# Softmax reciprocals from GpSimd to VectorE, and one group of adaLN rows from the first channel mixer to the second token mixer

## The chip, the cores and the metric

The kernel runs on one core of a Trainium2 (trn2) chip. The metric is the device time of one execution in microseconds (us), and what counts is the median of several executions. In the text, TensorE, VectorE, ScalarE, GpSimd and SyncE are the five engines; the profile calls them PE (with PEld for its weight loads), DVE, ACT, POOL and SP.

## What is computed

Two layers of a conditioned decoder trunk run over 256 tokens of width 1024. All is fp32. Cut to its structure, the reference is:

```python
c_act = silu(c)
for l in range(2):
    mod = c_act @ w_mod[l] + b_mod[l]                      # six adaLN rows of 1024
    sh1, sc1, g1, sh2, sc2, g2 = split(mod, 6)
    h = rms_norm(x, mix_norm_g[l]) * (1 + sc1) + sh1
    x = x + g1 * token_mixer(h, ...)                       # attention A, attention B, conv, gates, w_out
    h = rms_norm(x, ffn_norm_g[l]) * (1 + sc2) + sh2
    x = x + g2 * channel_mixer(h, ...)                     # w_up, 3-tap conv, silu(a)*b, w_down
```

The token mixer projects `h` once and has three branches: a latent attention (8 heads), a second attention (8 heads, which with 256 tokens is plain causal attention), and a gated causal convolution of 31 taps over 512 channels. The three branches are weighted by sigmoid gates, summed and projected by `w_out`. Softmax divides each row of exponentials by its sum; the reciprocal of that sum is what the first part of the change is about. Row (l, r) below is the r-th of the six adaLN rows of layer l: (1,2) is `g1` of the second layer, the gate with which the token mixer's output is added to `x`.

## The kernel before

Tokens stand in the free dimension, channels on the 128 partitions, so `x` is eight tiles of 128x256. Products in fp32 are made of three matmuls each: both factors are split into a rounded part (hi, type fp32r) and the rest (lo), and hi·hi, lo·hi and hi·lo are accumulated in PSUM (lines 281 to 291).

Weights come in units of 512 KB. SyncE loads a unit to `raw` (line 194, 4 buffers), ScalarE rounds it to `whi` (line 211), VectorE subtracts to get `wlo` (line 213), and TensorE uses both. Units are taken three ahead of their use (`AHEAD = 3`).

Each engine executes its list of instructions in order. The lists follow from the order in which the program's parts are written, with a scheduler at build time that fixes each engine's list. The order of the parts in a token mixer is written out by hand in `STEPS`, one string for each layer. Of its names, `MA` and `BA` are parts of the two attentions, `C` and `G` gates, `O` and `OC` output products of the branches, `PR` the last projection. A pair in small letters marks a stretch over which a list of small pieces is spread evenly (`_spread`): `v0`..`v1` the conv taps, `m0`..`m1` parts of rows that are made by matmul, and `r0`..`r1` adaLN rows that VectorE makes.

An attention group (`attn4`, line 555) has four heads. TensorE makes the scores, VectorE takes the maxima (lines 582 and 584) and their scaled negatives `nb` (lines 588 and 591), ScalarE takes exponentials with their sums `sm` (line 604), and then comes the reciprocal of 128x4 sums, two for each group, 16 in all:

```python
ri = small(4, "ri", 4)
if RIP:
    gp.tensor_tensor(ri, sm, minus1[:, 0:4], op=ALU.pow)
```

ScalarE multiplies the probabilities with it (line 619), TensorE transposes them (line 628) and multiplies with the values (line 640), and the result is split to `oah`, `oal` or `obh`, `obl` (lines 643 and 644). The conv taps are VectorE operations of 128x256 (lines 1012 and 1015), which are spread among the attention groups.

An adaLN row (l, r) takes eight steps k. In each, SyncE loads 512 KB of `wmr` (line 366) and VectorE multiplies it by `crow`, which is silu(c) laid out over all partitions, and sums (line 371); a small addition of the bias follows (line 372). `crow` is made by `row_load`: a load (step `RW0`, line 1132), a tanh on ScalarE (line 1135) and a product on VectorE (line 1136, step `RW3`). It stands in the pool "kv" with 2 buffers, and in the token mixer the rows' loads have 2 buffers of the pool "qkT". In the kernel before, rows (0,3) and (0,4) are made in the first layer's token mixer (`RPARTS`), and rows (1,0), (1,1) and (1,2) in the first channel mixer.

The channel mixer has 22 groups of 256 columns. `up(j)` makes a group in PSUM (`psb`, 3 buffers, two units of weights), ScalarE takes it from there (line 1192), VectorE adds the taps (line 1194), and after the activation (lines 1199 and 1200) the product is split to `mh` and `ml` (lines 1202 and 1203). At its end stand the rows of the first layer:

```python
for _ in range(2 if j % 7 == 6 else j > 0):
    if rows_left:
        mod_row(crow1[0], *rows_left.pop(0), scale=0.5 if CDMA else 1.0)
```

There they have four loading buffers of their own. `down(j)` multiplies with the down weights, 24 matmuls to 48 in `up`, so 72 a group and 1584 in a channel mixer. `up` runs three groups ahead of `down`, and the last three `down` are issued together (`TAIL = 3`, lines 282 to 284). The new `x` follows from them (line 1226). `g1h` (line 1144) is where the second layer's token mixer uses row (1,2), after its last projection.

Of the kernel before, what the change touches and what calls it, by code (L numbers as in the profile page):

```python
# [9 lines left out]
F32 = mybir.dt.float32  # L10
# [4 lines left out]
ALU = mybir.AluOpType  # L15
AX = mybir.AxisListType

P = 128
S = 256
NB = 2  # L20
D = 1024
KD = 8
# [8 lines left out]
VFROM = [("QKV", 2, 0), ("KL", 0)]  # L31
TAPS = 4
SQP = 0
RIP = 1
LNAT = {"LN": 16, "LS": 18, "LB": 20}
PB = 4
DVN = ()
# [6 lines left out]
CDMA = 1  # L44
# [1 line left out]
HOLD = 0  # L46
SQ4 = 1
CHAIN = 1
RPARTS = [(0, 3), (0, 4)]
RFROM = ("G", 5, 0)  # L50
RTO = ("PR", 5)
MFROM = ("QKV", 2, 0)
# [3 lines left out]
LINE = 512  # L56
LEAD = 16
TAILP = 2
FLEAD = 1
ROWS = [(0, 0), (0, 1), (1, 0), (1, 1), (1, 2)] + RPARTS  # L60


PARTS = [[(0, r) for r in (2, 3, 4) if (0, r) not in RPARTS], [(1, 4)]]
# [19 lines left out]
)]  # L83


def _spread(o, items, first, last):

    i0, i1 = o.index(first), o.index(last)
    total = sum(UNITS.get(t[0], 0) for t in o[i0:i1])
    res, done, n = [], 0, 0  # L90
    for i, t in enumerate(o):
        res.append(t)
        if i0 <= i < i1:
            done += UNITS.get(t[0], 0)
            while n < len(items) and done >= total * (n + 0.5) / len(items) - 1e-9:
                res.append(items[n])
                n += 1
    return res


def _order(l):
    o = []
    for w in STEPS[l].split():
        name = w.rstrip("0123456789")
        o.append((name, *(int(d) for d in w[len(name):])))
    o = _spread(o, [("V", j, t, min(31, t + TAPS)) for j in range(4) for t in range(0, 31, TAPS)], ("v", 0), ("v", 1))
    if ("r", 0) in o:
        o = _spread(o, [("R", r, k) for _, r in RPARTS for k in range(KD)], ("r", 0), ("r", 1))
    o = _spread(o, [("M",)] * (9 * len(PARTS[l])), ("m", 0), ("m", 1))
    return [t for t in o if t[0].isupper() and not (l == 0 and C0K and t[:2] == ("C", 0))]  # L110

# [37 lines left out]
def trunk_kernel(ctx, tc, xT, crow, ccol, pos, invf, modb_d, cols_d, grow_d, wmr, wm, win1, wqkv,  # L149
                  wgc, wgab, wuq, wukv, woab, woc, wout, wup, wdn, out):  # L150
    nc = tc.nc
    te, ac, ve, gp, sy = nc.tensor, nc.scalar, nc.vector, nc.gpsimd, nc.sync

    cst = ctx.enter_context(tc.tile_pool(name="cst", bufs=1))
    per = ctx.enter_context(tc.tile_pool(name="per", bufs=1))
    wk = ctx.enter_context(tc.tile_pool(name="wk", bufs=2))
# [4 lines left out]
    def nm(s):  # L161
        uid[0] += 1
        return f"{s}_{uid[0]}"
# [149 lines left out]
    ve.memset(mean_w, 1.0 / 512.0)  # L313
    mhalf = cst.tile([P, 24], F32, name="mhalf")
    ve.memset(mhalf, -0.5)

    minus1 = cst.tile([P, 4], F32, name="minus1")
    ve.memset(minus1, -1.0)


    def silu_row(res, tag="thc", bufs=1):
# [53 lines left out]
    def mod_row(row, l, r, k, tag=None, scale=1.0):  # L375

        return use_row(wload_row(l, r, k, tag), row, l, r, k, scale)
# [177 lines left out]
    def attn4(qT, kT, v, scale, scq, oth, otl, oslot, apart=False):  # L555
# [39 lines left out]
        for i in range(2):  # L595
            sm = small(4, "smx", 4)
            ps = []
            for h in (2 * i, 2 * i + 1):
                pr = wk.tile([P, 384], F32, tag="p", name=nm("p"), bufs=PB)
                for b in range(NB):  # L600
                    src = (at0 if b == 0 else at1)[h]
                    at = h % 2 * 2 + i
                    dst = pr[:, 0:P] if b == 0 else pr[:, P:384]
                    ac.activation(dst, src, AF.Exp, bias=nb[:, b, at:at + 1],  # L604
                                  scale=scale if scq is None else scq[b][:, h:h + 1],
                                  accum_out=sm[:, len(ps):len(ps) + 1])
                    ps.append(dst)
            ri = small(4, "ri", 4)
            if RIP:
                gp.tensor_tensor(ri, sm, minus1[:, 0:4], op=ALU.pow)  # L610
            else:
                ve.reciprocal(ri, sm)
            prs.append((ps, ri))
        for ps, ri in prs:
            for n, pr in enumerate(ps):
# [54 lines left out]
    def layer(l):  # L670
# [455 lines left out]
        def row_load(n):  # L1126

            if not CDMA:
                return step(rowgen, 2 if n == 3 else 1)
            if n == 0:  # L1130
                crow1.append(wk.tile([P, D + 128], F32, tag="kv", name=nm("crow"), bufs=2, align_bytes=LINE)[:, 0:D])
                sy.dma_start(crow1[0], crow)
            elif n == 3:
                th = wk.tile([P, D], F32, tag="qkT", name=nm("th"), bufs=2, align_bytes=LINE)
                ac.activation(th, crow1[0], AF.Tanh, scale=0.5)
                ve.scalar_tensor_tensor(crow1[0], th, 1.0, crow1[0], op0=ALU.add, op1=ALU.mult)

        run["RW"] = row_load
        run["R"] = lambda r, k: mod_row(crow1[0], 0, r, k, "qkT", 0.5 if CDMA else 1.0)
        for tok in CFG["order"][l]:  # L1140
            run[tok[0]](*tok[1:])
        step(mods, 99)
# [19 lines left out]
            ve.tensor_scalar(fb[:, NF:44], cv(l, "fdw_b")[:, NF:44], 0.5, None, op0=ALU.mult)  # L1162
        acc2 = []
        acts = []
        rows_left = [(1, r, k) for r in range(3) for k in range(KD)] if l == 0 else []

        def down(j):
            if not acc2:
# [10 lines left out]
        def up(j):  # L1179
# [22 lines left out]
            ac.activation(mh, th, AF.Copy)  # L1202
            ve.tensor_tensor(ml, th, mh.bitcast(F32), op=ALU.subtract)
            acts.append((mh, ml))
            for _ in range(2 if j % 7 == 6 else j > 0):
                if rows_left:
                    mod_row(crow1[0], *rows_left.pop(0), scale=0.5 if CDMA else 1.0)
            if l + 1 < L and j == 6:
                load_cols(l + 1)
                prepare(l + 1)  # L1210
# [107 lines left out]
```

## Time and profile before

| | before |
|---|---|
| times of three runs | 961.74, 956.33, 953.44 us; median 956.33 |
| profiled execution | 960.24 us, of it span 958.4 us |
| mean granted clock of TensorE in the span | 0.979 |
| TensorE matmuls (PE) busy | 910.8 us, 95% |
| TensorE weight loads (PEld) busy | 852.6 us, 89% |
| VectorE (DVE) busy | 792.0 us, 83% |
| ScalarE (ACT) busy | 553.7 us, 58% |
| GpSimd (POOL) busy | 81.9 us, 9% |
| read from memory | 198.81 MB, mean 209 GB/s |

The span runs from the first to the last instruction of the profiled execution; times in the trace count from its start. The first layer's token mixer adds to `x` from 287.9 us on (line 1146), its channel mixer from 487.0 us (line 1226), and the last addition to `x` of the second token mixer starts at 757.3 us. Matmuls are pipelined, so a busy share near 100% says that TensorE isn't starved, not that it runs at its peak. The granted clock is given as a share of 2.4 GHz, so 0.5 is 1.2 GHz. Shares over the whole span mix stages with different limits, and so stretches of 10 to 40 us are read below.

### The profile page before, as it was taken

How to read it: one execution, taken by the hardware profiler on the slowest of the kernel's cores; microseconds unless marked ns; L12 is line 12 of the kernel's file. 1: busy time of each engine (PE TensorE's matmuls, PEld its weight loads, DVE VectorE, ACT ScalarE, POOL GpSimd, SP SyncE). 2: the span in 40 equal slices, each digit the busy share in tenths (PEclk: the TensorE clock that was granted, in tenths of full speed). 3: DMA queues.
4: the chain of work that ended last, by engine and by line, in shares of the span. 5: the costliest groups of instructions: out<-in, count | busy, mean ns of one | idle time of the engine just before them, and what ended most of it. 6: DMA issues, size and time to landing. Idle time of an engine off the chain costs nothing.

```text
span 958.4 us, 18539 instructions
## 1 busy us (share of the span) xinstructions
PE 910.8 (95%) x7262; PEld 852.6 (89%) x7262; DVE 792.0 (83%) x1524; ACT 553.7 (58%) x978; POOL 81.9 (9%) x48
## 2 busy tenths in 40 slices
PE   3999899799999999999899999979999999999998
PEld 2998788798997999999879987769999899999998
DVE  5999799799997899998874999967677798777774
ACT  4577488634655555555643675847565566555551
POOL 1011621300000000000000042231000000000000
PEclk9999999999998999999979999979999999999999
DMA  7966434388896878888753665505557767656641
GB/s 255 388 218 216 140 111 138 125 271 303 289 323 227 287 252 287 294 309 265 227 184 103 193 221 186 176 23 176 189 167 229 264 210 219 185 190 181 193 134 44
DMA packets 58120, 201.07 MB, mean 210 GB/s; under 512 B 6960, under 2 KB 8496, under 8 KB 58032
## 3 DMA queue, kind: packets, MB, share of 16 engines
q1 hardware_dynamic: 58032, 199.88, 62.4%
q8 instruction: 57, 0.93, 0.4%
q14 instruction: 31, 0.25, 0.1%
HBM read 198.81 MB, written 1.05 MB: 209 GB/s over the span
## 4 chain that ended last, share of the span: by engine, by line
PE 68%; DVE 11%; issue 8%; DMA 5%; POOL 4%; ACT 3%; SPq 0%; POOLq 0%; DVEq 0%; ACTq 0%
PE psb L288 13%; PE psb L291 13%; PE psb L289 13%; PE psa L288 6%; PE psa L289 6%; PE psa L291 6%; DVE wlo L213 3%; POOL rs L470 2%; DVE cacc L1015 2%; PE psa L388 2%; DMA raw<-in_wmr 2%; POOL ri L610 2%; ACT p L604 2%; DVE raw L371 1%; PE psa L628 1%
## 5 line engine op out<-in xcount | busy, mean ns | idle before, releaser
L211 ACT ACTIVATE whi<-raw 128x1024 fp32r<-128x1024 f32 (+2 forms) x286 | 294.4, 1037 | 217.0 <-PE psb L289 100.4
L213 DVE TENSOR_TENSOR wlo<-raw,whi 128x1024 fp32r<-128x1024 f32 (+2 forms) x286 | 340.4, 1194 | 82.6 <-ACT whi L211 71.4
L288 PE MATMUL psb<-hh,whi 128*128 128x256 f32 x1088 | 263.6, 283 | 1.2 <-ACT p L604 0.8
L289 PE MATMUL psb<-hl,whi 128*128 128x256 f32 x1088 | 260.8, 280 | 0.0
L288 PEld LDWEIGHTS psb<-hh,whi 128*128 128x128 f32 x1088 | 205.3, 189 | 9.1 <-issue 4.9
L289 PEld LDWEIGHTS psb<-hl,whi 128*128 128x128 f32 x1088 | 205.1, 189 | 1.4 <-DVE hl L534 1.1
L291 PE MATMUL psb<-hh,wlo 128*128 128x256 f32 x1088 | 150.5, 280 | 0.0
L291 PEld LDWEIGHTS psb<-hh,wlo 128*128 128x128 f32 x1088 | 136.8, 189 | 0.9 <-issue 0.8
L1015 DVE SCALAR_TENSOR_TENSOR cacc<-upad,cw,cacc 128x256 f32<-128x256 f32 x240 | 105.0, 480 | 0.4
L470 POOL TENSOR_TENSOR rs<-rs,mhalf 128x16 f32<-128x16 f32 (+3 forms) x22 | 48.8, 2228 | 585.6 <-DVE rs L469 581.5
L288 PE MATMUL psa<-mhl,whi 128*128 128x256 f32 x400 | 95.2, 279 | 0.0
L289 PE MATMUL psa<-mhl,whi 128*128 128x256 f32 x400 | 95.0, 279 | 0.0
L1194 DVE SCALAR_TENSOR_TENSOR e<-psb,fw,e 128x255 f32<-128x255 f32 (+1 forms) x176 | 83.9, 478 | 10.9 <-ACT e L1192 9.7
L288 PEld LDWEIGHTS psa<-mhl,whi 128*128 128x128 f32 x400 | 75.2, 189 | 0.2 <-ACT mhl L1096 0.2
L289 PEld LDWEIGHTS psa<-mhl,whi 128*128 128x128 f32 x400 | 75.2, 188 | 0.0
L1192 ACT ACTIVATE e<-psb,fb,fw 128x256 f32<-128x256 f32 x88 | 48.6, 553 | 34.9 <-DVE e L1194 21.1
L291 PE MATMUL psa<-mhl,wlo 128*128 128x256 f32 x400 | 54.6, 279 | 0.0
L371 DVE SCALAR_TENSOR_TENSOR raw<-raw,crow 128x1024 f32<-128x1024 f32 x40 | 48.7, 1218 | 2.9 <-DMA raw<-in_wmr 2.9
L291 PEld LDWEIGHTS psa<-mhl,wlo 128*128 128x128 f32 x400 | 50.1, 189 | 0.0
L610 POOL TENSOR_TENSOR ri<-smx,minus 128x4 f32<-128x4 f32 x16 | 31.5, 1978 | 93.2 <-ACT p L604 93.2
L288 PE MATMUL psb<-whi,hh 128*128 128x416 f32 (+1 forms) x96 | 32.0, 355 | 7.6 <-ACT hh L765 7.6
L388 PE MATMUL psa<-raw,cact 128*32 128x256 f32 x320 | 32.7, 445 | 0.4 <-DMA raw<-in_wm 0.4
(267 smaller groups left out, 1509.7 us busy)
## 6 DMA issues: line engine op xcount, KB each, us to landing
raw<-in_wup SPq DMA_DIRECT2D x88, 512.0 KB, 4.7
raw<-in_wmr SPq DMA_DIRECT2D x56, 512.0 KB, 5.2
raw<-in_wdn SPq DMA_DIRECT2D x44, 512.0 KB, 4.2
raw<-in_wm SPq DMA_DIRECT2D x40, 512.0 KB, 4.4
raw<-in_wgab SPq DMA_DIRECT2D x32, 512.0 KB, 4.7
raw<-in_wqkv SPq DMA_DIRECT2D x24, 512.0 KB, 4.8
raw<-in_win SPq DMA_DIRECT2D x16, 512.0 KB, 4.8
raw<-in_wgc SPq DMA_DIRECT2D x16, 512.0 KB, 4.2
```

The source lines that it names most:

```text
L211: ac.activation(hi, raw, AF.Copy)
L213: ve.tensor_tensor(lo, raw, hi.bitcast(F32), op=ALU.subtract)
L288: te.matmul(o, p1[0], p1[1], start=start, stop=False)
L289: te.matmul(o, p2[0], p2[1], start=False, stop=False)
L291: te.matmul(o, p3[0], p3[1], start=False, stop=stop)
L371: ve.scalar_tensor_tensor(raw, raw, scale, row, op0=ALU.mult, op1=ALU.mult, accum_out=acc)
L388: te.matmul(acc[32 * c:32 * c + 32, 0:S], cact[:, k:k + 1].to_broadcast([P, 32]), raw[:, c * S:(c + 1) * S], start=(k == 0), stop=(k == KD ...
L470: gp.tensor_tensor(r, r, mhalf[:, :n], op=ALU.pow)
L610: gp.tensor_tensor(ri, sm, minus1[:, 0:4], op=ALU.pow)
L1015: ve.scalar_tensor_tensor(aj, upad[:, j, t:t + S], cw[:, j * 31 + t:j * 31 + t + 1], aj, op0=ALU.mult, op1=ALU.add)
L1192: ac.activation(t, src, AF.Identity, scale=fw[:, 2, c:c + 1], bias=fb[:, c:c + 1])
L1194: ve.scalar_tensor_tensor(t[:, d:S], src[:, 0:S - d], fw[:, 2 - d, c:c + 1], t[:, d:S], op0=ALU.mult, op1=ALU.add)
```

## The change

The change has two parts. First, the 16 reciprocals of the softmax sums are made on VectorE with its reciprocal operation, and the GpSimd power with its constant `minus1` goes. Second, row (1,2) leaves the first channel mixer's list and is spread, like (0,3) and (0,4) in the first layer, over a stretch `r0`..`r1` of the second layer's token mixer, behind a new load of `crow` (`RW0` to `RW3`). The channel mixer's remaining 16 row steps come one a group from j = 2 on. `wmr` holds the rows in the order of `ROWS`, so its blocks are put in another order. Line numbers of the changed kernel are 1 to 7 lower from there on.

```diff
-RIP = 1
...
-RPARTS = [(0, 3), (0, 4)]
+RPARTS = [(0, 3), (0, 4), (1, 2)]
...
-ROWS = [(0, 0), (0, 1), (1, 0), (1, 1), (1, 2)] + RPARTS
+ROWS = [(0, 0), (0, 1), (1, 0), (1, 1)] + RPARTS
...
-    "BA12 C30 G11 C31 BA13 O0 O1 G20 LN G21 G30 G31 O2 G40 G41 G50 O3 LS G51 LB G60 O4 O5 G61 OC0 G70 OC1 PR0 "
-    "OC2 OC3 PR1 OC4 OC5 G71 O6 O7 PR2 OC6 PR3 OC7 PR4 PR5 PR6 PR7 "
+    "BA12 C30 G11 C31 BA13 O0 O1 G20 RW0 LN G21 G30 RW1 RW2 RW3 G31 O2 G40 r0 G41 G50 O3 LS G51 LB G60 O4 O5 G61 "
+    "OC0 G70 OC1 PR0 OC2 OC3 PR1 OC4 OC5 G71 O6 O7 PR2 OC6 PR3 r1 OC7 PR4 PR5 PR6 PR7 "
...
-        o = _spread(o, [("R", r, k) for _, r in RPARTS for k in range(KD)], ("r", 0), ("r", 1))
+        o = _spread(o, [("R", r, k) for n, r in RPARTS if n == l for k in range(KD)], ("r", 0), ("r", 1))
...
-            if RIP:
-                gp.tensor_tensor(ri, sm, minus1[:, 0:4], op=ALU.pow)
-            else:
-                ve.reciprocal(ri, sm)
+            ve.reciprocal(ri, sm)
...
-                crow1.append(wk.tile([P, D + 128], F32, tag="kv", name=nm("crow"), bufs=2, align_bytes=LINE)[:, 0:D])
+                crow1[:] = [wk.tile([P, D + 128], F32, tag="kv", name=nm("crow"), bufs=2, align_bytes=LINE)[:, 0:D]]
...
-        run["R"] = lambda r, k: mod_row(crow1[0], 0, r, k, "qkT", 0.5 if CDMA else 1.0)
+        run["R"] = lambda r, k: mod_row(crow1[0], l, r, k, "qkT", 0.5 if CDMA else 1.0)
...
-        rows_left = [(1, r, k) for r in range(3) for k in range(KD)] if l == 0 else []
+        rows_left = [(1, r, k) for r in range(2) for k in range(KD)] if l == 0 else []
...
-            for _ in range(2 if j % 7 == 6 else j > 0):
-                if rows_left:
-                    mod_row(crow1[0], *rows_left.pop(0), scale=0.5 if CDMA else 1.0)
+            if j > 1 and rows_left:
+                mod_row(crow1[0], *rows_left.pop(0), scale=0.5 if CDMA else 1.0)
```

The three places below show how the lists of the engines move. A row is a line of the program, the operation, the tile written and the tiles read, and the shape; x16 stands for 16 alike in a row.

The first is VectorE in the first layer's last attention group, where `cacc` are the conv taps. Before:

```order
L213 TENSOR_TENSOR wlo_1971<-raw_1968,whi_1970 128x1024
L1015 SCALAR_TENSOR_TENSOR cacc_1234<-upad_749,cw_738,cacc_1234 128x256 x4
L1012 TENSOR_SCALAR cacc_1234<-upad_749,cw_738,col_178 128x256
L1015 SCALAR_TENSOR_TENSOR cacc_1234<-upad_749,cw_738,cacc_1234 128x256 x16
L213 TENSOR_TENSOR wlo_2030<-raw_2027,whi_2029 128x1024
```

And the same place after the change:

```order
L212 TENSOR_TENSOR wlo_1969<-raw_1966,whi_1968 128x1024
L1008 SCALAR_TENSOR_TENSOR cacc_1232<-upad_747,cw_736,cacc_1232 128x256 x3
L605 RECIPROCAL ri_1886<-smx_1879 128x4
L1008 SCALAR_TENSOR_TENSOR cacc_1232<-upad_747,cw_736,cacc_1232 128x256
L1005 TENSOR_SCALAR cacc_1232<-upad_747,cw_736,col_176 128x256
L1008 SCALAR_TENSOR_TENSOR cacc_1232<-upad_747,cw_736,cacc_1232 128x256 x2
L605 RECIPROCAL ri_1895<-smx_1888 128x4
L1008 SCALAR_TENSOR_TENSOR cacc_1232<-upad_747,cw_736,cacc_1232 128x256 x13
L212 TENSOR_TENSOR wlo_2028<-raw_2025,whi_2027 128x1024
```

The two reciprocals of the group now stand among the taps, the second behind two taps of the long run and ahead of 13.

The second is VectorE in the second layer from the last attention group on, where `wlo` is a split of a gate's weights, `e` the first step of the conv's layer norm, and `gs` the gain of the next norm. Before:

```order
L1015 SCALAR_TENSOR_TENSOR cacc_6933<-upad_6456,cw_4272,cacc_6933 128x256
L540 SCALAR_TENSOR_TENSOR gs_9228<-mod_101,col_4258 128x8
L1015 SCALAR_TENSOR_TENSOR cacc_6933<-upad_6456,cw_4272,cacc_6933 128x256 x11
L213 TENSOR_TENSOR wlo_7877<-raw_7874,whi_7876 128x1024
L1026 TENSOR_TENSOR e_1407_8177<-cacc_6933 128x256
L213 TENSOR_TENSOR wlo_7917<-raw_7914,whi_7916 128x1024
```

And after the change, where L1129 is the product that makes `crow` and L367 a row:

```order
L1008 SCALAR_TENSOR_TENSOR cacc_6891<-upad_6414,cw_4260,cacc_6891 128x256
L605 RECIPROCAL ri_7813<-smx_7806 128x4
L1129 SCALAR_TENSOR_TENSOR crow_8133<-th_8209,crow_8133 128x1024
L1008 SCALAR_TENSOR_TENSOR cacc_6891<-upad_6414,cw_4260,cacc_6891 128x256
L605 RECIPROCAL ri_7822<-smx_7815 128x4
L367 SCALAR_TENSOR_TENSOR raw_8371,m_1423_8373<-raw_8371,crow_8133 128x1024
L1008 SCALAR_TENSOR_TENSOR cacc_6891<-upad_6414,cw_4260,cacc_6891 128x256
L368 TENSOR_TENSOR mod_99<-m_1423_8373,modb 128x1
L536 SCALAR_TENSOR_TENSOR gs_9231<-mod_99,col_4246 128x8
L1008 SCALAR_TENSOR_TENSOR cacc_6891<-upad_6414,cw_4260,cacc_6891 128x256 x3
L367 SCALAR_TENSOR_TENSOR raw_8458,m_1439_8460<-raw_8458,crow_8133 128x1024
L212 TENSOR_TENSOR wlo_7835<-raw_7832,whi_7834 128x1024
```

The product for `crow` and the first two rows come in among the taps of the last attention group; a third row stands a few instructions further, ahead of the subtraction that makes the group's `obl` (L644 before, L637 after).

The third is SyncE in the second layer's token mixer, where `in_wgc`, `in_wgab` and `in_woab` are weights of gates and outputs, and `in_wmr` those of the rows. Before:

```order
L194 DMA raw_7774<-in_wgab 128x1024
L194 DMA raw_7808<-in_wgc 128x1024
L194 DMA raw_7874<-in_wgab 128x1024
L194 DMA raw_7914<-in_wgc 128x1024
L194 DMA raw_7969<-in_woab 128x1024
L194 DMA raw_7999<-in_woab 128x1024
L194 DMA raw_8031<-in_wgab 128x1024
```

And after the change:

```order
L193 DMA raw_7832<-in_wgab 128x1024
L1125 DMA crow_8133<-in_crow 128x1024
L193 DMA raw_7872<-in_wgc 128x1024
L193 DMA raw_8371<-in_wmr 128x1024
L193 DMA raw_7927<-in_woab 128x1024
L193 DMA raw_7957<-in_woab 128x1024
L193 DMA raw_8458<-in_wmr 128x1024
L193 DMA raw_8602<-in_wmr 128x1024
L193 DMA raw_8696<-in_wmr 128x1024
L193 DMA raw_7989<-in_wgab 128x1024
```

The load of `crow` and four loads of rows come in among the weights of the gates and outputs.

Two more moves have no rows here. In VectorE's list of the first channel mixer the last row (L371 before, L367 after) stands before the 16th L1203 in the kernel before and before the 11th L1196, which is the same line, after. On ScalarE, the tanh for `crow` (L1128 after) stands in the second layer behind the `oah` of an attention group (L636), and one gate step (L729) stands between it and the next group's exponentials.

## Rows read from the trace of the kernel before

**Rows 1.** Stretches: us, PE, PEld, DVE, ACT, POOL busy (instructions), clock, DMA, GB/s.
```profile
192.00:216.00 24.00, 23.85 (x210) 22.57 (x209) 24.00 (x42) 9.14 (x10) 0.00 (x0) 1.00 0.82 273
432.00:456.00 24.00, 24.00 (x214) 24.00 (x213) 21.05 (x39) 13.43 (x22) 0.00 (x0) 1.00 0.79 262
648.00:672.00 24.00, 24.00 (x221) 23.70 (x220) 18.60 (x29) 18.94 (x41) 2.46 (x2) 1.00 0.52 173
840.00:864.00 24.00, 24.00 (x206) 24.00 (x205) 17.86 (x30) 14.07 (x21) 0.00 (x0) 1.00 0.58 182
```

**Rows 2.** Line 610, ns shortest/median/longest, first to last; below, who waits for it.
```profile
L610 POOL TENSOR_TENSOR ri<-smx,minus x16: 1003/1316/6367, 123.5 to 652.7; 128x4 f32<-128x4 f32 x16
...
  ACT p L619: 11.7, 6
```

**Rows 3.** Timeline, first layer's last attention group: start, us, engine, instruction, [wait <-releaser].
```profile
170.68 6.42 DVE L1015 SCALAR_TENSOR_TENSOR cacc<-upad,cw,cacc 128x256 f32<-128x256 f32 x16
171.60 6.37 POOL L610 TENSOR_TENSOR ri<-smx,minus 128x4 f32<-128x4 f32 x1 [0.29 <-ACT p L604]
178.46 0.48 PE L628 MATMUL psa<-ident,p 128*128 128x128 f32 x1 [5.04 <-ACT p L619]
182.68 1.23 DVE L213 TENSOR_TENSOR wlo<-raw,whi 128x1024 fp32r<-128x1024 f32 x1 [5.58 <-ACT whi L211]
```

**Rows 4.** Timeline, an attention group of the second layer.
```profile
628.10 7.21 DVE L1015 SCALAR_TENSOR_TENSOR cacc<-upad,cw,cacc 128x256 f32<-128x256 f32 x18
630.15 6.03 POOL L610 TENSOR_TENSOR ri<-smx,minus 128x4 f32<-128x4 f32 x1 [0.70 <-ACT p L604]
636.66 0.47 PE L628 MATMUL psa<-ident,p 128*128 128x128 f32 x1 [4.70 <-ACT p L619]
643.68 0.42 DVE L582 TENSOR_REDUCE mx<-psa 128x2 f32<-128x256 f32 x1 [8.38 <-PE psa L573]
```

**Rows 5.** Stretches behind two of TensorE's waits.
```profile
632.00:648.00 16.00, 11.34 (x60) 8.11 (x61) 6.90 (x16) 5.44 (x11) 4.17 (x1) 0.68 0.04 7
476.00:488.00 12.00, 8.15 (x42) 7.54 (x43) 10.46 (x20) 6.42 (x12) 0.00 (x0) 0.72 0.72 225
```

**Rows 6.** Timeline of ScalarE and TensorE, end of the first channel mixer.
```profile
444.53 0.55 ACT L1192 ACTIVATE e<-psb,fb,fw 128x256 f32<-128x256 f32 x1
...
470.90 1.07 PE L291 MATMUL psb<-hh,wlo 128*128 128x256 f32 x8
...
479.41 0.58 PE L282 MATMUL psa<-mhl,whi 128*128 128x256 f32 x1 [4.03 <-ACT mhl L1202]
...
480.21 0.55 ACT L1192 ACTIVATE e<-psb,fb,fw 128x256 f32<-128x256 f32 x1
```

**Rows 7.** Lines 591 and 371, as in rows 2.
```profile
L591 DVE SCALAR_TENSOR_TENSOR nb<-mx,scb x8: 154/156/160, 147.6 to 646.4; 128x4 f32<-128x4 f32 x8
...
L371 DVE SCALAR_TENSOR_TENSOR raw<-raw,crow x40: 1211/1218/1228, 202.5 to 438.0; 128x1024 f32<-128x1024 f32 x40
```

**Rows 8.** DMA issues: queue, count, KB of each, median us from issue to landing.
```profile
raw<-in_wmr SPq DMA_DIRECT2D x56, 512.0 KB, 5.2
...
crow<-in_crow SPq DMA_DIRECT2D x1, 512.0 KB, 3.6
```

**Rows 9.** Timeline of ScalarE: the tanh for crow, first layer, and an attention group, second layer.
```profile
161.19 1.05 ACT L1135 ACTIVATE th<-crow 128x1024 f32<-128x1024 f32 x1
...
621.00 0.60 ACT L643 ACTIVATE oah<-psa 128x512 fp32r<-128x512 f32 x1 [0.40 <-PE psa L640]
...
625.95 0.46 ACT L604 ACTIVATE p<-psa,nb,scb 128x128 f32<-128x128 f32 x1 [1.48 <-DVE nb L591]
```

**Rows 10.** Stretches of the second token mixer, columns as in rows 1.
```profile
650.40:666.70 16.30, 16.30 (x153) 15.99 (x152) 13.22 (x22) 14.41 (x31) 2.46 (x2) 1.00 0.49 147
650.40:690.00 39.60, 39.60 (x356) 39.24 (x355) 28.93 (x43) 25.13 (x45) 2.46 (x2) 1.00 0.56 182
```

**Rows 11.** Timeline of TensorE: the first matmul that reads the last obl.
```profile
667.08 0.28 PE L289 MATMUL psb<-obl,whi 128*128 128x256 f32 x1
```

More of the change, by code (lines that the diff above doesn't have):

```diff
@@ L315, in trunk_kernel @@
     ve.memset(mhalf, -0.5)
-    minus1 = cst.tile([P, 4], F32, name="minus1")
-    ve.memset(minus1, -1.0)
     def silu_row(res, tag="thc", bufs=1):
```

## The prediction

> **What bounds the kernel now.** I read the share of busy time first (95% of the span for TensorE), then stretches, then what TensorE waits for, and the timelines there. With TensorE busy nearly always, only what stands on its path can be won, and the stretches tell which stage has room [rows 1]. In the first channel mixer (432 to 456 us) TensorE is full, 214 matmuls in 24 us, and VectorE has 3 us to spare: work taken from VectorE there wins nothing by itself. After the first layer's attention (192 to 216 us) VectorE is the fuller one. After the second layer's attention (648 to 672 us) TensorE is full and VectorE has 5.4 us of 24 free. So the change takes work from a stage that doesn't wait in its middle, and adds it to one that has some room.
>
> TensorE's long waits are then three, and all touch the change. Sixteen reciprocals run on GpSimd, with a median of 1.32 us and a longest of 6.37, and ScalarE's normalisations wait for them, 11.7 us in total [rows 2]. In the first layer the long one runs from 171.60 to 177.97, while VectorE does 16 conv taps without a gap; it ends 0.9 us after the last tap. TensorE's transposes stand 5.04 us for it, and VectorE's own next step 5.58 us [rows 3]. In the second layer it is 6.03 us beside 18 taps, TensorE is idle for 4.70 us, and VectorE's next maximum stands for 8.38 us [rows 4]. Behind such a stall the granted clock falls from 2.4 to 1.2 GHz for a while: over 632 to 648 us its mean is 0.68, over 476 to 488 us 0.72 [rows 5].
>
> The third wait is at the end of the first channel mixer: the last `down` matmuls stand 4.03 us for the activation of `up(20)`. TensorE had finished `up(21)` at 472.0 (470.90 plus 1.07), yet ScalarE takes it from PSUM at 480.21: it runs 8.2 us behind [rows 6].
>
> **The change part by part.**
>
> *Reciprocals in the first layer.* Eight GpSimd powers go; eight VectorE reciprocals of 128x4 come. The trace has no reciprocal on VectorE. An operation on 128x4 takes 0.16 us there [rows 7]; the far ends are nothing and GpSimd's median, 1.32. I take 0.16, since engine and size are the same. In the new list the second reciprocal of the stalled group stands behind two taps of that run instead of racing all 16, so it can start at 171.5 (170.68 plus two of 0.40), when its sums are there: GpSimd had started at 171.60. The 5.04 us go, and VectorE's 5.58 with them. What the lower clock costs behind it I don't count: VectorE has no slack there (24.00 of 24 us [rows 1]). Gain 5.0, bounds 3 and 6.
>
> Here a rule speaks against the size of this. GpSimd is held through 16 and 18 taps [rows 3, 4]. The Trainium skill, "SBUF — State Buffer", section "Who interferes with whom", says that a VectorE instruction with two SBUF inputs and a GpSimd instruction that reads SBUF share a port pair, and that whoever starts first keeps it for that whole instruction. By that rule a reciprocal is held up for one tap, 0.40 us, and the two long ones would be accidents of this execution, which others needn't have; the rows don't agree with it. What accidents would mean is worked out among the rivals.
>
> *Reciprocals in the second layer.* The same, with 4.70 us of waiting and then a lower clock, (1 - 0.68) x 16 = 5.1 us, together 9.8. But from there the chain goes through VectorE's maximum for the last group, which can come forward only by the 8.38 us that it waits. Gain 8.4, bounds 4.7 and 9.8.
>
> *The other 14 reciprocals.* Of ScalarE's 11.7 us the two long ones make some 10, so 1.7 us are left [rows 2]. Against that stand 16 x 0.16 = 2.6 us more on VectorE, and a reciprocal that waits for its sums holds all behind it: taps, splits of weights, maxima, for which TensorE waits. I take +0.5, bounds -2 and +1.7.
>
> *Row (1,2) leaves the first channel mixer.* Eight loads of 512 KB go from SyncE, and eight products of 1.22 us from VectorE [rows 7], 10 us. TensorE waited for none of them in the middle, so they win nothing there. The end is different. From `up(16)`, taken at 444.53, to `up(21)` at 480.21 there are no rows (the last began at 438.0 [rows 7]), and ScalarE takes a group every 7.14 us, where TensorE needs 72 matmuls at 24/214, or 8.07 us: it catches up 0.93 us a group [rows 1, 6]. In the new VectorE list the last row stands before the 11th activation, not the 16th. Five more groups at 0.93 are 4.7 us, more than the 4.03 that TensorE waited. So the wait goes, and what the clock costs behind it, (1 - 0.72) x 12 = 3.4 us [rows 5], together 7.4. I take 7.0, as the margin is thin; bounds 0 and 7.4.
>
> *Row (1,2) enters the second token mixer.* It brings `crow` once more, with its tanh and product, and eight loads and products. The load of `crow` stands on SyncE before a gate weight, and needs a buffer that TensorE reads until just before 621.00, where ScalarE takes that result [rows 9]; it lands 3.6 us later [rows 8], and its tanh of 1.05 us [rows 9] ends at 625.7. One more ScalarE step of 0.6 us follows, then the exponentials of the next group, at 625.95 before: they slip by 0.3 to 0.6 us. I take -0.6, bounds 0 and -1.9 (if it lands as late as a row's load, after 5.2). On VectorE the crow product and three rows, 4 x 1.22 = 4.9 us, stand before the last `obl`, and in 650.4 to 666.7 us VectorE has 16.3 - 13.2 = 3.1 us free [rows 10]. So `obl` comes 1.8 us late, and TensorE, which read it at once, at 667.08 [rows 11], waits; a little more if a row waits for its load (5.2 us to landing [rows 8]). I take -2.1, bounds 0 and -6. Of the other five rows nothing hangs but splits of weights that are three units ahead. If that cover is gone, each row costs its 1.2 us, 6 us in all.
>
> **Sum.** 5.0 + 8.4 + 0.5 + 7.0 - 0.6 - 2.1 = 18.2 us. The profiled execution took 960.24 us (span 958.4 and 1.8 around it), so 942.0. The median of the runs is 956.33, 3.9 lower; 18.2 off that is 938.1. I take 940, between them.
>
> **The rivals.**
>
> *The long reciprocals are accidents,* and the median run has one of the two. For it: 14 of 16 are short, and the runs spread over 8 us (953.4 to 961.7). Against: both long ones end 0.9 us after a run of taps. The two then win half of 13.4: 956.3 - 18.2 + 6.7 = 945. The rule on the port pair is the one that speaks for this.
>
> *The end of the first channel mixer keeps its wait.* For it: VectorE also splits weights of the next layer among the last groups. Against: it caught up wherever rows were absent. Without the 7 us: 940 + 7 = 947.
>
> *TensorE's pace.* The first channel mixer has 214 matmuls in 24 us, the second 206, both with TensorE full at the full clock [rows 1]; the cause I can't tell. If one of them flips, 1584 matmuls x (24/206 - 24/214) are 7 us: 947 or 933.
>
> *The rows starve the second mixer (slower).* Should the rows' loads come late, VectorE stands at each row, with splits, `obl` and PSUM reads behind it, and SyncE's queue with it. Eight waits of a whole load (5.2 us) are 42 us of VectorE; 10.7 us are free in 650.4 to 690 us [rows 10], and three units of weights ahead, 24 matmuls each, cover 8. That leaves 23 us: 940 + 23 = 963. It decides from some 19 us of such waits on. Against it: each load is issued two rows ahead, and other VectorE steps of 6 us lie between.
>
> **How the numbers follow.** Forecast 0.54, accidents 0.14, end kept 0.13, pace flipped to slow 0.11, starved 0.08. A measurement here tells about 1% from no change, so the limits are 946.8 and 965.9. The forecast's own range, 931 to 949, lies nearly all on the faster side; accidents and the kept end half; the slow pace a third; the starved case none, and most of it beyond 965.9 if the lower clock comes on top. That gives 0.70 faster, 0.24 same, 0.06 slower. The range, 930 to 955, leaves out the starved case and less than one in ten below.
>
> **What would show it.** Right: no reciprocal on GpSimd; transposes (now L621) waiting under 1 us each; no clock of 0.50 in the second layer's attention or at the end of the first channel mixer; and a new TensorE wait of about 2 us on `obl` in the second layer. Wrong: VectorE standing at its reciprocals or at the second layer's rows for several us each, or the last `down` matmuls still waiting 4 us.

## The result, and the profile after

| | before | changed |
|---|---|---|
| first comparison, median of 4 runs each | 954.88 us (953.17 to 961.74) | 935.37 us (927.8 to 945.01) |
| ratio, 95% interval | | 0.974 (0.969 to 0.979) |
| second comparison, 17 and 6 runs | 958.06 us (953.75 to 964.16) | 936.42 us (931.07 to 939.92) |
| ratio, 95% interval | | 0.978 (0.974 to 0.981) |
| profiled execution; span | 960.24; 958.4 us | 933.22; 931.3 us |

The change makes the kernel 2.2 to 2.6% faster, by 19.5 and 21.6 us of the medians. The two profiled executions lie 27.0 us apart. The ratios, here and below, leave out executions over 1.5% above the fastest of their kernel, which the medians keep: 945.01 us here, and below one of 948.03 (reciprocals alone), one of 1479 (rows held back) and one of 2265 (two orders more).

To see where, I paired each TensorE instruction of the trace before with the same one in every other trace, and took the time between two such instructions as the length of a stage. The first row names the stages by the times of before; all numbers are us. Four of the kernels are told of below.

| TensorE from .. to | 130..168 | 168..194 | 256..292 | 310..470 | 470..505 | 600..624 | 624..650 | 650..690 | 790..940 |
|---|---|---|---|---|---|---|---|---|---|
| before | 38.0 | 25.96 | 35.98 | 159.97 | 34.99 | 24.20 | 25.55 | 40.06 | 150.05 |
| changed | 36.92 | 19.00 | 39.30 | 159.94 | 26.97 | 24.20 | 16.20 | 41.82 | 150.05 |
| changed, once more | 36.93 | 19.01 | 39.81 | 160.03 | 26.51 | 24.20 | 16.22 | 42.04 | 144.39 |
| reciprocals alone | 36.94 | 19.44 | 38.43 | 161.22 | 34.09 | 24.30 | 15.99 | 40.07 | 144.39 |
| row alone | 38.43 | 26.30 | 36.43 | 166.00 | 26.63 | 24.29 | 26.75 | 40.58 | 144.39 |
| without row (1,2) | 36.95 | 19.02 | 38.66 | 161.55 | 26.56 | 24.20 | 15.98 | 40.06 | 150.05 |
| two orders more | 36.93 | 19.40 | 34.65 | 159.98 | 26.95 | 24.20 | 16.10 | 40.24 | 150.05 |

Three stages are 7 to 9 us shorter (168..194, 470..505, 624..650), and two are longer: 256..292 by 3.3 and 650..690 by 1.8.

The reciprocals of the changed kernel, by line, and under them who waits for them:

```profile
L605 DVE RECIPROCAL ri<-smx x16: 164/171/179, 120.0 to 624.5; 128x4 f32<-128x4 f32 x16
...
  ACT p L612: 1.1, 1
```

Against [rows 2] the longest is 0.18 us in place of 6.37, and ScalarE waits 1.1 us in place of 11.7. The timeline of the first layer's last attention group shows its second reciprocal, in the place of the long power:

```profile
166.82 0.17 DVE L605 RECIPROCAL ri<-smx 128x4 f32<-128x4 f32 x1
166.91 5.21 DVE L1008 SCALAR_TENSOR_TENSOR cacc<-upad,cw,cacc 128x256 f32<-128x256 f32 x13
...
167.83 0.28 PE L621 MATMUL psa<-ident,p 128*128 128x128 f32 x1
```

It stands ahead of the 13 taps, and the transposes go on among them, without the wait of [rows 3]. Stretches of the changed kernel show the granted clock there and in the two others (columns as in [rows 1]):

```profile
168.00:192.00 24.00, 24.00 (x222) 23.10 (x222) 23.78 (x42) 14.22 (x21) 0.00 (x0) 1.00 0.54 186
...
460.00:472.00 12.00, 11.87 (x103) 11.63 (x102) 8.75 (x18) 5.55 (x11) 0.00 (x0) 1.00 0.48 153
604.00:620.00 16.00, 14.81 (x129) 12.89 (x128) 16.00 (x41) 12.35 (x33) 0.00 (x0) 1.00 0.27 92
```

It is 1.00 in all three; behind the stalls of before it was 0.72 and 0.68 [rows 5], and 0.93 over 168 to 192 us of before:

```profile
168.00:192.00 24.00, 18.96 (x159) 18.14 (x158) 17.59 (x35) 14.43 (x33) 8.05 (x2) 0.93 0.38 125
```

The end of the first channel mixer in the changed kernel, ScalarE and TensorE:

```profile
460.69 1.07 PE L290 MATMUL psb<-hh,wlo 128*128 128x256 f32 x8
461.86 0.55 ACT L1185 ACTIVATE e<-psb,fb,fw 128x256 f32<-128x256 f32 x1
```

ScalarE takes the last group 0.1 us after TensorE's last matmul ends (460.69 + 1.07), where it was 8.2 us behind [rows 6]; the wait is gone.

The stage that became longer at 256..292 has a wait that [rows 3 to 6] have nothing of. VectorE and TensorE at the end of the first token mixer of the changed kernel:

```profile
270.57 1.22 DVE L367 SCALAR_TENSOR_TENSOR raw<-raw,crow 128x1024 f32<-128x1024 f32 x1 [1.82 <-DMA raw<-in_wmr]
...
272.18 0.42 DVE L1087 TENSOR_TENSOR e<-e,mq 128x256 f32<-128x256 f32 x1
```

```profile
269.97 1.07 PE L290 MATMUL psa<-mhl,wlo 128*128 128x256 f32 x8
273.10 0.39 PE L281 MATMUL psa<-mhl,whi 128*128 128x256 f32 x1 [2.07 <-ACT mhl L1089]
```

The last adaLN row of the first layer waits for its load, a step of the last merged branch (L1087, for the operand `mhl`) is queued behind it on VectorE, and TensorE stands 2.07 us for that. The same row before:

```profile
281.13 1.23 DVE L371 SCALAR_TENSOR_TENSOR raw<-raw,crow 128x1024 f32<-128x1024 f32 x1 [1.15 <-DMA raw<-in_wmr]
```

VectorE waited for it there too. But TensorE's matmuls ahead of this place (269.97, before 282.74) now come 12.8 us earlier, and the row only 10.6 us. With the reciprocals alone the stage is 2.5 us longer than before, with the row alone 0.5, so it is mainly the earlier attention that shows this wait.

### The profile page after: what moved, and what is told of

The parts are those of the page before. It is cut to its first block, busy times and chain, and to the rows that moved or that the text cites. A ratio compares the mean times of both kernels' runs of the same rounds, so it can differ in the third digit from the quotient of the medians.

```text
span 931.3 us, 18548 instructions
## 1 busy us (share of the span) xinstructions
PE 897.1 (96%) x7262; PEld 844.8 (91%) x7262; DVE 793.5 (85%) x1540; ACT 554.0 (59%) x979; POOL 45.8 (5%) x32
## 4 chain that ended last, share of the span: by engine, by line
PE 80%; DVE 10%; DMA 4%; issue 2%; ACT 2%; POOL 2%; SPq 0%; POOLq 0%; DVEq 0%; ACTq 0%
PE psb L287 16%; PE psb L288 15%; PE psb L290 15%; PE psa L287 8%; PE psa L288 8%; PE psa L290 8%; DVE wlo L212 3%; DMA raw<-in_wmr 3%; DVE cacc L1008 2%; PE psa L384 2%; POOL rs L466 2%; PE psa L621 1%; DVE raw L367 1%; PE psa L281 1%; PE psa L633 1%
## 5 line engine op out<-in xcount | busy, mean ns | idle before, releaser
L466 POOL TENSOR_TENSOR rs<-rs,mhalf 128x16 f32<-128x16 f32 (+3 forms) x22 | 44.3, 2022 | 688.7 <-DVE rs L465 687.9
L367 DVE SCALAR_TENSOR_TENSOR raw<-raw,crow 128x1024 f32<-128x1024 f32 x40 | 48.7, 1218 | 5.8 <-DMA raw<-in_wmr 5.8
L1195 ACT ACTIVATE mhl<-e 128x256 fp32r<-128x256 f32 x44 | 18.3, 417 | 27.0 <-DVE e L1193 26.2
L287 PE MATMUL psa<-hh,whi 128*128 128x256 f32 x128 | 30.8, 285 | 0.0
```

Source lines behind the costliest of these rows:

```text
L287: te.matmul(o, p1[0], p1[1], start=start, stop=False)
L367: ve.scalar_tensor_tensor(raw, raw, scale, row, op0=ALU.mult, op1=ALU.mult, accum_out=acc)
L466: gp.tensor_tensor(r, r, mhalf[:, :n], op=ALU.pow)
```

## The experiments

**Each part alone.** The kernel before with `RIP = 0` has the reciprocals on VectorE and leaves row (1,2) where it was; the changed kernel with the power (and its constant `minus1`) has the row moved alone:

```diff
-            ve.reciprocal(ri, sm)
+            gp.tensor_tensor(ri, sm, minus1[:, 0:4], op=ALU.pow)
```

> The kernel before with the reciprocals on VectorE; row (1,2) stays in the first channel mixer. The forecast's terms (5.0 + 8.4 + 0.5): 14 us less than before, some 941, no GpSimd step in the softmax, no clock of 0.5 in either attention, and the wait of 4 us at the end of the first channel mixer still there. If the two long reciprocals were accidents of the profiled execution: 7 us less or fewer, 948 or more.

> The changed kernel with the power on GpSimd again; row (1,2) is in the second token mixer. The forecast's terms (7.0 - 0.6 - 2.1): 4 us less than before, some 951, the wait at the end of the first channel mixer gone, and in its trace two reciprocals of 6 us again, each as long as a run of conv taps. If the long ones were accidents, the trace has them elsewhere or not at all, and the time is nearer to that of the changed kernel.

Measured on one chip beside 958.06 us before: reciprocals alone 942.71 us (ratio 0.981, 0.976 to 0.986), the row alone 951.65 (0.995, 0.992 to 0.998), both 936.42. That is 15.4 and 6.4 us, and their sum, 21.8, is what both give, 21.6. The intervals are some 3 to 5 us wide to either side, and within that the parts don't interfere. In the trace of the row alone the long powers stand where they stood before. By line:

```profile
L607 POOL TENSOR_TENSOR ri<-smx,minus x16: 1003/1414/6346, 120.5 to 649.9; 128x4 f32<-128x4 f32 x16
```

And in its timeline:

```profile
168.82 6.03 DVE L1010 SCALAR_TENSOR_TENSOR cacc<-upad,cw,cacc 128x256 f32<-128x256 f32 x15
169.37 6.35 POOL L607 TENSOR_TENSOR ri<-smx,minus 128x4 f32<-128x4 f32 x1 [0.32 <-ACT p L602]
```

6.35 against 6.37 us, ending again 0.87 us after the last tap (169.37 + 6.35 against 168.82 + 6.03), and a second one of 6.03 us in the second layer, as before. They belong to the order of the kernel, not to one execution. In the trace of the reciprocals alone, TensorE's waits from 460 to 480 us still have that of the end of the first channel mixer, shorter than the 4.03 of before (total, times, longest):

```profile
PE psa L282 <- ACT mhl L1202: 2.8, 2, 2.1
```

**What row (1,2) costs where it is now.** The kernel without the row empties two functions in the second layer, and its gate takes another row there; one of the three edits:

```diff
-        run["RW"] = row_load
+        run["RW"] = row_load if l == 0 else (lambda n: None)
```

> The changed kernel without row (1,2): its crow, its eight loads and its eight products are left out, and the second layer's gate is taken from another row. By the forecast (0.6 + 2.1) it is 2.7 us faster than the changed kernel. If VectorE's busy time counts there (9 steps of 1.2 us): 11 us faster. If the rows are quite hidden: no faster.

> The changed kernel once more beside the three others. Some 935 us; its trace has the wait on the last obl (0.8 us) and the wait of 2 us at the end of the first token mixer again, if they belong to the kernel and not to one execution.

Measured: 935.55 us without the row, 936.42 with it. The difference of 0.9 us is less than the medians can tell; 11 us, as much as VectorE works on the row, is excluded. By the stages it costs some 2 us: 650..690 is 2.0 us shorter without it (40.06 against 42.04) and 624..650 0.2 us (15.98 against 16.22). Most of it lies at the wait on `obl`, which both traces of the changed kernel have:

```profile
PE psb L288 <- DVE obl L637: 0.8, 1, 0.8
...
PE psb L288 <- DVE obl L637: 1.5, 1, 1.5
```

In the first of them TensorE waits another 0.5 us for `obh` beside it. What follows, 690..764, takes 73.1 to 74.8 us in the traces of the table, with the row and without it, so that no gain or loss there can be put down to the row. The wait at the end of the first token mixer is in both executions too (256..292: 39.30 and 39.81).

**Where the rows of the first channel mixer stand.** The same 16 rows, held back behind the split `ml` of their group (`mli` is that instruction).

```diff
-            if j > 1 and rows_left:
-                mod_row(crow1[0], *rows_left.pop(0), scale=0.5 if CDMA else 1.0)
+            for _ in range(2 if j > 13 and rows_left else 0):
+                t = rows_left.pop(0)
+                raw = wload_row(*t)
+                with tc.issue_after(mli.ins):
+                    use_row(raw, crow1[0], *t, 0.5 if CDMA else 1.0)
```

> The changed kernel with the same 16 rows of the first channel mixer, held back: two for each group from the 14th on. If what counts at its end is how far ScalarE stands behind TensorE there (two rows make a group 7.14 + 2.44 = 9.6 us against 8.07), it is some 12 us behind at group 20, the last products wait 3 us and the lower clock follows: 6 us slower than the changed kernel, some 942. If the number of rows counts (16 in place of 24): no wait and no difference.

> The kernel with the held rows once more, for its trace: the last products of the first channel mixer wait about 3 us for the activation, ScalarE is some 12 us behind TensorE at group 20, and the granted clock falls to 0.5 behind it. If the number of rows is what counts: none of this.

Measured: 944.04 us (0.986, 0.983 to 0.989), as the first reading said, but in the trace of the repeat (947.6 us) not for its reason: the last products wait 0.3 us, not 3. ScalarE takes group 20 at 465.57, 2.8 us behind TensorE's last matmul of it (461.66 + 1.10), not 12. Some half of the loss is elsewhere. The rows share their four loading buffers with the loads of `in_wm` for the next layer's start. SyncE issues the last two rows at 474.6 us and six loads of `in_wm` only from 482.1, and TensorE waits for those (its waits from 466 to 490 us in that trace):

```profile
PE psa L384 <- DMA raw<-in_wm: 1.5, 1, 1.5
...
PE psa L281 <- ACT mhl L1195: 0.3, 1, 0.3
```

So 470..505 is 4 us longer than in the changed kernel (30.50 against 26.51), and 310..470 takes 166.04 by the slower pace told of below, which need not come from the edit; the rest of the loss stays open. How fast two rows push ScalarE back was misjudged: over 432 to 456 us VectorE does 22.85 us of work in 24, so it has time for both. The slower pace helps it, 72 x 117.8 ns or 8.5 us a group; no trace has these rows at the faster one.

**What holds the power on GpSimd.** Four kernels. The first three do nothing but powers beside runs of VectorE operations.

> Nothing of the trunk is computed: 27 powers of 128x4 on GpSimd, each started together with a run of VectorE operations, and the input is copied to the output. If a run of conv taps holds GpSimd for its whole length, the power takes about 0.4 us for each tap behind which it stands: 6 us beside 16 taps, 13 beside 32, near 1.3 beside 2 or none. If it is held for one tap at most: under 2 us beside every run. Runs of 16 operations with one input in SBUF, or with the other in PSUM, tell which kind of operation holds it.

> Again only powers and VectorE runs, the trunk left out. In the first bench each tap waited for the one before and began 0.04 us after its end; in the kernel two chains of taps take turns and each begins some 0.09 us before the other's end. If it is the missing pause that holds GpSimd, the power takes as long as a run of taking turns: 0.4 us a tap, 6 us beside 16, 13 beside 32, 3 where a run of 16 is broken in the middle, and 1.0 beside one chain of 16. If it isn't, all are near 1 again and the long powers of the kernel have another cause.

> The bench with one thing changed: the power is set off by a small ScalarE copy, so that it starts inside the run, as in the kernel, and no longer at its first tap. If a run of taps without a pause holds off a power that comes after its start, the power ends some 0.9 us after the last tap: 6 to 7 us beside 16 taps of two chains, 13 beside 32, and 1 to 2 beside one chain of 16, which pauses. Runs of one SBUF input, and a run with such an operation at every fourth place, should let it in. If the powers are near 1 us once more, neither the run nor its start explains the kernel's long ones.

All three came out the other way: every power took 1.01 to 1.27 us, beside every kind of run. A place of the timelines of the second and third, with 16 taps:

```profile
20.51 6.46 DVE L184 SCALAR_TENSOR_TENSOR acc<-u,smtwosixteena,acc 128x256 f32<-128x256 f32 x16
20.56 1.01 POOL L178 TENSOR_TENSOR ritwosixteena<-smtwosixteena,minus 128x4 f32<-128x4 f32 x1 [2.59 <-DVE smtwosixteena L173]
```

```profile
20.95 1.07 POOL L178 TENSOR_TENSOR ritwosixteena<-latetwosixteena,minus 128x4 f32<-128x4 f32 x1 [2.50 <-ACT latetwosixteena L177]
```

They have taps at the kernel's own spacing (16 in 6.46 us, 6.42 in [rows 3]). So the fourth goes back into the kernel:

```diff
+            ve.tensor_scalar(small(4, "brk", 2), aj[:, 0:4], 1.0, None, op0=ALU.mult)
```

> The kernel before, power on GpSimd, with a small operation of one input (128x4) on VectorE behind every four conv taps of a channel group, and behind the finished trunk a bench on the kernel's own tiles: powers that start 0 to 8 small ScalarE copies into a run of 32 taps, and beside three other runs. Its time isn't comparable. In the trunk: if an unbroken run of two-input operations is what holds the power, no power of 128x4 takes over 2.5 us and TensorE's waits at the transposes fall from 10 us to under 3; if the run isn't the cause, there are powers of 6 us again. In the bench: if a power is held only when it comes some taps after the run's start, those behind 3 or more copies last to 0.9 us after the run, up to 12 us, and the early ones 1 us; if the bench has no long ones, the cause is still open.

In the trunk the expectation holds. The powers of the softmax by line, and who waits for them:

```profile
L610 POOL TENSOR_TENSOR ri<-smx,minus x16: 1003/1144/2261, 121.4 to 663.3; 128x4 f32<-128x4 f32 x16
...
  ACT p L619: 1.3, 2
```

The longest is 2.26 us, ScalarE's wait falls from 11.7 to 1.3 us, and TensorE's at the transposes from 9.7 at the two long ones alone [rows 3, 4] to 4.7 at all of them (the expectation said 3). With the run broken the long powers go, so the run is part of their cause. The small operation isn't the only difference, though: the scheduler set VectorE's list anew, and no power of this kernel starts with more than four taps of an unbroken run left. Nor is a run enough. In the trace before, two powers stand beside ten taps without a gap and end 1.9 us ahead of the last:

```profile
152.76 3.00 POOL L610 TENSOR_TENSOR ri<-smx,minus 128x4 f32<-128x4 f32 x2 [9.21 <-ACT p L604]
153.62 4.04 DVE L1015 SCALAR_TENSOR_TENSOR cacc<-upad,cw,cacc 128x256 f32<-128x256 f32 x10
```

The second of them, of 1.21 us, started with eight taps of the run left; both long ones had 14. In the bench behind the trunk the 14 powers beside two-input taps, started 0 to 8 copies into the run, took 1.0 to 1.33 us; but one beside a run of one-input operations, in both rounds, lasted to its end (timeline):

```profile
1068.90 7.96 DVE L1254 TENSOR_SCALAR bacc<-bacc,smoneina 128x256 f32<-128x256 f32 x30
1069.90 7.00 POOL L1275 TENSOR_TENSOR rioneina<-lateaonein,minus 128x4 f32<-128x4 f32 x1 [9.75 <-ACT lateaonein L1272]
```

A power can thus be held to the end of an unbroken run, and mostly isn't. The one in the bench ends with the run (1076.90 against 1076.86), those of the kernel 0.87 us behind it, so that they need not be held by the same thing. What decides between 1 us and the whole run is open.

The Trainium skill, "SBUF — State Buffer", section "Who interferes with whom", lets two-input operations contend and one-input operations outside a two-port mode not, with a lock for one instruction. The bench's powers beside two-input taps agree with it: at most 0.33 us over the shortest, less than one tap of 0.40. The kernel's long ones don't: GpSimd was held through 14 further taps and not one. The operations that held a power in the bench had one input; whether they ran in a two-port mode no run shows.

**Two orders more.** From the two new waits a version follows: in the second token mixer the product for `crow`, and so all rows, behind the last `obl`; in the first, the last row behind the last split. The second of these also ran alone.

```diff
+                with tc.issue_after(lastlo[0].ins) if l else ExitStack():
+                    ve.scalar_tensor_tensor(crow1[0], th, 1.0, crow1[0], op0=ALU.add, op1=ALU.mult)
...
+            with tc.issue_after(lastml[0].ins) if (l, r, k) == (0, 4, KD - 1) else ExitStack():
+                use_row(raw, crow1[0], l, r, k, 0.5 if CDMA else 1.0)
```

> The changed kernel with two orders added on VectorE: in the second token mixer the product for crow and with it all rows stand behind the last obl, and in the first token mixer the last row stands behind the last split of the merged branches. The wait on obl (0.8 to 1.5 us) and that at the end of the first token mixer (2.1 to 2.9 us, with a lower clock behind it) go: 4 us faster than the changed kernel, 932. If the loads of the rows are the limit in both places, the waits only move: no faster.

> The second of those two orders alone (the last row of the first token mixer behind the last split): 3 us faster than the changed kernel, with the wait of TensorE at the end of the first token mixer under 1 us. If the split was late for another reason: no faster, and the wait stays.

Measured beside 956.51 us before: 931.96 with both (0.973, 0.970 to 0.975), 933.31 with the second alone (0.975, 0.972 to 0.978). In the trace with both, VectorE's timeline has the last split (of `mhl`) first and the row after it:

```profile
273.08 0.42 DVE L1091 TENSOR_TENSOR mhl<-e,mhl 128x256 fp32r<-128x256 f32 x1
273.42 1.22 DVE L367 SCALAR_TENSOR_TENSOR raw<-raw,crow 128x1024 f32<-128x1024 f32 x1
```

TensorE's wait there is down to 0.2 us. 256..292 falls from 39.3 to 34.65 us, under that of before, and 650..690 from 41.8 to 40.24. In the trace with the second order alone they are 34.64 and 41.95: each order takes back its own wait. By the ratios the two give 1 to 5 us more than the changed kernel; the intervals touch its own, so by time alone that is likely rather than shown.

## Why the prediction was right, point by point

The forecast was 940 us; 935.4 and 936.4 were measured, inside the range of 930 to 955, and the gain was 19.5 and 21.6 us against 18.2. That the sum came so near is in part luck: all four gains came out larger than forecast, and a loss of 3.3 us that the forecast hadn't took some of that back.

*Reciprocals in the first layer:* 5.0 forecast, 7.0 by the stage (25.96 to 19.0), above the bound of 6. The step that was off is "what the lower clock costs behind it I don't count": the clock counted, (1 - 0.93) x 24 = 1.7 us in 168 to 192 us. VectorE being full further on (24.00 of 24 us) didn't take it back there. It was taken back in part at the end of the first token mixer, 3.3 us, by a wait that the forecast didn't have: the last row's load. Before, VectorE waited 1.15 us for it, and TensorE's longest wait there was 0.72. The prediction has GpSimd held through 16 and 18 taps; the powers started inside the runs, and it was 14 both times.

*Reciprocals in the second layer:* 8.4 forecast, 9.35 measured in 624..650 (25.55 to 16.20), within the bounds.

*The other 14:* +0.5 forecast; 130..168, where four of them stand, gained 1.1, and nothing with the row alone (38.43 against 38.0). The new wait of VectorE at its reciprocals is small, 1.2 us in three places.

*Row (1,2) leaves the first channel mixer:* 7.0 forecast; 8.0 in 470..505, and 8.4 in the trace of the row alone, above the bound of 7.4. The middle of the mixer is unchanged (159.97 and 159.94), as forecast. The catching up is borne out. Measured as in [rows 6], from the end of a group's last matmul to ScalarE's first read of it, ScalarE before is furthest behind at group 16, 13.4 us, and 8.2 at group 21, 1.0 us less a group; in the changed kernel it is 8.7 us behind at group 12, behind the last row, and 0.1 from group 19 on, 1.2 us less a group. The held rows showed that its rate with rows isn't simply 1.22 us a row more.

*Row (1,2) enters the second token mixer:* the slip of the exponentials, -0.6, didn't come. They start 4.94 us behind `oah` (602.43 and 607.37), before 4.95 (621.00 and 625.95 [rows 9]), since the load of `crow` came early enough for the tanh and the gate step (L729) to end at 607.25, when VectorE's `nb` is done too (607.12 + 0.15). But the tanh held that gate step back, which empties a PSUM buffer, and TensorE waits 1.2 us for it, a wait that the forecast didn't have (from the timelines of ScalarE and VectorE and from TensorE's waits, in the changed kernel):

```profile
605.71 1.06 ACT L1128 ACTIVATE th<-crow 128x1024 f32<-128x1024 f32 x1 [2.68 <-DMA crow<-in_crow]
606.67 0.58 ACT L729 ACTIVATE thc<-psb 128x512 f32<-128x512 f32 x1
607.37 0.46 ACT L600 ACTIVATE p<-psa,nb,scb 128x128 f32<-128x128 f32 x1
...
607.12 0.15 DVE L587 SCALAR_TENSOR_TENSOR nb<-mx,scb 128x4 f32<-128x4 f32 x1
...
PE psb L287 <- ACT thc L729: 1.2, 1, 1.2
```

Little is left of that wait: 624..650, where it lies, takes 16.20 and 16.22 us with the row and 15.98 without it; there TensorE waits 0.9 us for the exponentials instead. The late `obl`, -2.1, came as -1.8 to -2.0 in its stage.

The sum of the terms as measured, 7.0 + 9.35 + 1.1 + 8.0 - 3.3 - 1.8, is 20.4 us. I don't count the other 6.6 us between the profiled executions as the change's, though no run shows what they are: 3.6 of them lie ahead of 130 us, nearly all ahead of the first reciprocal, and the profiled execution of before took longer than 18 of its 21 timed runs in these two comparisons.

*The rivals.* The long reciprocals were no accidents: they recur at the same places. The end kept its wait only where the row stayed. The rows didn't starve the second token mixer; VectorE waited for their loads 0.96 us at one row there and 0.82 at another, in the changed kernel's trace. TensorE's pace does flip, more often than a chance of 0.11 says, but the table has either pace with each part of the change and without it, so it isn't tied to the change.

*The signs.* No reciprocal is left on GpSimd, the clock is 1.00 at both places named, and the last `down` matmuls don't wait. The wait on `obl` is 0.8 and 1.5 us in place of about 2. One transpose waits longer than the 1 us that was allowed, in the first attention group of the first layer, where the reciprocal comes at 119.98 us behind other steps of VectorE's list:

```profile
PE psa L621 <- ACT p L612: 1.9, 1, 1.9
```

In the second trace of the changed kernel that wait is 0.2 us. And the prediction calls three waits TensorE's long ones; the trace before has others of 3 to 7.6 us, the longest near its start for `hh`, which the change doesn't touch.

## What to carry to other kernels

A small step on GpSimd between two stages of a softmax can be held through a run of VectorE operations; where VectorE can do the step itself in 0.17 us, put it between them. Taking work from VectorE won here at the end of the channel mixer, where ScalarE had to catch up, and not in its middle. Where a stage becomes earlier, look which load or row was hidden by its lateness, and let an instruction that waits for a load stand behind those that TensorE waits for.

## What the hardware showed that I had not expected

TensorE has two paces at the full clock. In the second channel mixer every trace of the table has one of two lengths for 790..940, 150.05 or 144.39 us, and the matmuls of 128x256 start 117.8 or 113.3 ns apart. The same stretch of the changed kernel, twice:

```profile
840.00:864.00 24.00, 24.00 (x206) 24.00 (x206) 18.29 (x30) 13.58 (x20) 0.00 (x0) 1.00 0.57 182
```

```profile
840.00:864.00 24.00, 24.00 (x214) 24.00 (x213) 18.78 (x30) 13.98 (x21) 0.00 (x0) 1.00 0.62 195
```

It is 206 or 214 matmuls in 24 us with the same program and granted clock. In ten traces of the trunk the pace changes only at an interruption, a gap of 153 ns or more between two matmuls, and often stays as it was behind one. In the trace of the reciprocals alone one matmul came 153 ns after the one before at 428.5 us, and from there the spacing was 117.8 in place of 113.3 ns to the end of the mixer. Over a channel mixer it is 6 us, and over two mixers 12, as much as the timed runs of before spread (953.17 to 964.16 us); how much of that spread is pace, the times alone don't tell. Which pace follows an interruption stays open.
